# Splitting three of four block products of the second plain tile into float32r parts

## The chip, the cores and the metric

The kernel runs on 1 core of one Trainium2 chip. The metric is the device time of one execution in microseconds (us). Five engines work side by side, each through its own queue in order: TensorE (PE, with its weight loads PEld), VectorE (DVE), ScalarE (ACT), GpSimd (POOL) and SyncE (SP). SyncE issues plain DMAs, GpSimd the DMAs that add into their destination.

## The reference

One step of a decoder trunk in float32, over 512 new prompt rows and 8 sample rows (together NT = 520 columns here): a half-step SwiGLU FFN, a mixer of pooling heads and state-space heads, a second half-step FFN, a final norm. The change lies in the first FFN:

```python
def _rms_norm(x, g):
    xf = x.astype(jnp.float32)
    y = xf * lax.rsqrt(jnp.mean(xf * xf, axis=-1, keepdims=True) + EPS)
    return (y * g.astype(jnp.float32)).astype(x.dtype)

def _swiglu(x, wg, wu, wd):
    return (jax.nn.silu(x @ wg) * (x @ wu)) @ wd
...
    h = h + 0.5 * _swiglu(_rms_norm(h, ffn1_norm[l]), ffn1_w_gate[l], ffn1_w_up[l], ffn1_w_down[l])
```

x has 1024 features, the FFN 2816 hidden ones, which are 22 tiles of 128. The kernel keeps features on the 128 partitions: a matmul takes a 128x128 block of weights and 128 features of 260 columns (half of the 520).

## The kernel before

**Two forms of a product.** In float32 a product of a weight block and 260 columns is one matmul, which leaves two records in the profile. In split form (`mm3`, lines 121 to 126) weights and input are each held as a float32r number `hi` and a float32r remainder `lo`, and three float32r matmuls are added up: hi by hi (L122), hi by lo (L125), lo by hi (L126). The split needs work ahead: `hi` is a copy on ScalarE (L106), `lo` is either a subtraction on VectorE (L113) or a negated copy on ScalarE (L109) into which a DMA adds the weights from memory (L110, issued by GpSimd).

**Hidden tiles.** Most tiles of an FFN are done as units: a unit k (`load`, L329 to L353; `product`, L355 to L382) computes gate and up of a tile by seven block products instead of eight, which needs sums of weight blocks (L346 to L348) and of input blocks. `raw_k` is a unit's weights as loaded (L340), one of two buffers; `whi`, `wlo`, `shi`, `slo` are the split weights and sums, `A` and `BE` the PSUM banks, L380 the copies out of them. The names end in the tile's number and a letter for the part: `slo_1d` is the remainder of the second pair of sums of unit 1, and unit 4 comes after unit 1.

**Plain tiles.** The first two tiles of the first FFN (0 and 3; `second` is 3) are done in float32 without sums (`plain`, L299 to L312): for gate (u = 0) and up (u = 1), over eight feature blocks (j of 0 to 3, q of 0 and 1) and two column halves b, that is 32 float32 matmuls for a tile. Each half of the columns and of the features has a slot of `xg`: `xg[:, 0]` and `xg[:, 1]` are the columns of half 0 with the features of q = 0 and 1, `xg[:, 3]` and `xg[:, 2]` those of half 1. The tiles' weights are `raw_0` and `raw_3`; `raw_1` follows in the buffer of `raw_0`.

**The start of the program** (L544 to L565). In a loop over j, SyncE loads two feature blocks of x and a quarter of tile 0's weights; ScalarE scales them into `xg` (L188) and squares them (L162), VectorE adds the squares (L163); tile 0's matmuls follow; `prep_pair` makes the seven inputs of the units as `xth` (hi, L201) and `xtl` (lo, L202), slots 0 to 2 of which are `xg`'s slots 0 to 2. After the loop come the loads of tile 3's weights (L293), `scales` (the sum of squares over partitions by two float32 matmuls `psr`, L168, square root on ScalarE, L169, reciprocal on VectorE, L170, giving `r`), tile 3's matmuls, and `plain_out` for both tiles (L314 to L327): the gate's banks times `r` (L319), silu on ScalarE (L321), times `r` (L322), times the up banks (L324). `g_split` (L247 to L285) makes the hidden values' sums and parts for the down projection.

**What sets the order.** A list scheduler places the instructions of each engine by its own estimate of time; what stands under `high_priority` goes first when it can. An engine then works through its queue in that order, waiting by semaphores. PSUM tiles and SBUF buffers with the same tag rotate, so a new one waits for the readers of an old one. Before the change tile 3's gate has the tag "A" and its up the tag "BE", the tags of the units; `psr` has the tag "ps".

## Time and profile before

| | us |
|---|---|
| median of three runs | 984.8 (984.1 to 984.87) |
| the profiled execution | 984.47 |
| its span in the trace | 982.6 |
| granted TensorE clock, share of full | 0.997 |

In a page of the profile, busy time is listed by engine; a row of the timeline gives start, length, engine, line, operation, tile written and tiles read, shape and count, and in brackets idle time before it and what ended it. A row of the stretches gives start and end, length, then the busy time of PE, PEld, DVE, ACT and POOL with counts, the granted clock, the share of time that the 16 DMA engines were busy, and GB/s. A row of DMA issues gives the tile, the queue, the count, the size of each and the median time from issue to landing. The chain of work that ended last is followed back from the end of the program: at each step to what released it, or to the instruction before it on its engine.

### The profile page before, as it was taken

What the parts mean: (1) busy time and instruction counts of PE and PEld (TensorE: products, weight loads), DVE (VectorE), ACT (ScalarE), POOL (GpSimd) and SP (SyncE); (2) the same over time, 40 slices, a digit from 0 to 9 for tenths busy, and PEclk for the clock granted to TensorE, in tenths of its full rate; (3) what the DMA queues carried; (4) which work ended last, traced back from release to release, by engine and by line L of the source; (5) the groups of instructions that cost most, each with busy time, mean ns of one, the idle gap of its engine ahead of it and who ended that gap; (6) DMA issues with size and microseconds to landing.
All of it is one profiled execution on the core that took longest, in us unless ns stands there. A gap on an engine that the chain in (4) does not pass through costs nothing.

```text
span 982.6 us, 20242 instructions
## 1 busy us (share of the span) xinstructions
PE 951.5 (97%) x7636; PEld 927.4 (94%) x7636; DVE 877.8 (89%) x1624; ACT 678.2 (69%) x1263; POOL 217.9 (22%) x319
## 2 busy tenths in 40 slices
PE   7999999999999999999999999999999999999995
PEld 6899999999999999999899998989999999999995
DVE  7899899989989698788979987999999999999976
ACT  7677677677777475685754335678788888888864
POOL 0112211121121000157411000113333233233300
PEclk9999999999999999999999999999999999999998
DMA  5565766576566243262335232456687768767732
GB/s 182 161 172 114 191 161 143 133 186 175 124 149 165 65 148 119 87 210 86 115 120 165 96 115 90 106 152 164 164 213 185 183 156 223 190 155 189 190 91 88
DMA packets 63571, 145.46 MB, mean 148 GB/s; under 512 B 9257, under 2 KB 22505, under 8 KB 63473
## 3 DMA queue, kind: packets, MB, share of 16 engines
q1 hardware_dynamic: 41168, 103.78, 33.2%
q0 software_dynamic: 22304, 40.38, 22.5%
q8 instruction: 60, 0.98, 0.4%
q14 instruction: 39, 0.31, 0.1%
HBM read 136.80 MB, written 7.34 MB: 147 GB/s over the span
## 4 chain that ended last, share of the span: by engine, by line
PE 85%; DVE 8%; ACT 3%; issue 2%; DMA 1%; POOL 1%; SPq 0%; DVEq 0%; ACTq 0%
PE A L126 7%; PE A L122 7%; PE A L125 7%; PE BE L122 6%; PE BE L125 6%; PE BE L126 6%; PE P L311 3%; PE wo L122 2%; PE wo L125 2%; PE wo L126 2%; PE inz L122 2%; PE A2d L125 2%; PE A2d L126 2%; PE A1d L125 2%; PE A1d L126 2%
## 5 line engine op out<-in xcount | busy, mean ns | idle before, releaser
L380 ACT COPY ac<-A 128x260 f32<-128x260 f32 x123 | 45.1, 369 | 16.8 <-PE A L126 16.5
L311 PE MATMUL P<-xg_f,raw 128*128 128x260 f32 x192 | 45.9, 398 | 5.5 <-DMA raw<-in_w1gu 5.5
L346 DVE TENSOR_TENSOR s<-raw 128x1024 f32<-128x1024 f32 x41 | 49.8, 1216 | 1.4 <-DMA raw<-in_w2gu 1.4
L311 PEld LDWEIGHTS P<-xg_f,raw 128*128 128x128 f32 x192 | 37.5, 199 | 11.5 <-ACT xg_f L188 5.4
L943 POOL DMA_DIRECT2D out_nss<-hs x32 | 20.6, 643 | 79.2 <-DVE hs L961 74.0
L106 ACT CAST whi_wo<-raw_wo 128x1024 fp32r<-128x1024 f32 x12 | 12.5, 1046 | 36.5 <-issue 9.2
L125 PE MATMUL wo<-catg,whi_wo 128*128 128x260 f32 x128 | 36.4, 285 | 1.3 <-DVE catg L1092 1.3
L122 PE MATMUL wo<-catg,whi_wo 128*128 128x260 f32 x128 | 37.3, 292 | 0.3 <-DVE h L1061 0.3
L122 PE MATMUL inz<-xh_mx,whi_inz 128*128 128x260 f32 x128 | 36.8, 288 | 0.0
L122 PE MATMUL inx<-xh_mx,whi_inx 128*128 128x260 f32 x128 | 36.4, 285 | 0.0
L126 PE MATMUL wo<-catg,wlo_wo 128*128 128x260 f32 x128 | 36.3, 284 | 0.0
L126 PE MATMUL inz<-xh_mx,wlo_inz 128*128 128x260 f32 x128 | 36.2, 283 | 0.0
L126 PE MATMUL inx<-xh_mx,wlo_inx 128*128 128x260 f32 x128 | 36.2, 283 | 0.0
L125 PE MATMUL inz<-xl_mx,whi_inz 128*128 128x260 f32 x128 | 36.2, 283 | 0.0
L125 PE MATMUL inx<-xl_mx,whi_inx 128*128 128x260 f32 x128 | 36.1, 282 | 0.0
L392 DVE TENSOR_TENSOR tg<-BE,ac 128x520 f32<-128x520 f32 x41 | 28.3, 691 | 5.2 <-PE BE L126 5.2
L807 DVE SCALAR_TENSOR_TENSOR A<-U,h,A 128x544 f32<-128x544 f32 x36 | 28.0, 778 | 4.3 <-ACT A L805 3.3
L401 DVE TENSOR_TENSOR tg<-tg,r_f 128x520 f32<-128x520 f32 x41 | 28.4, 694 | 1.3 <-ACT tg L399 1.0
L398 DVE TENSOR_TENSOR tg<-tg,r_f 128x520 f32<-128x520 f32 x41 | 28.4, 692 | 0.1
L347 DVE TENSOR_TENSOR s<-s,raw 128x512 f32<-128x512 f32 x41 | 28.0, 682 | 0.0
L348 DVE TENSOR_TENSOR s<-s,raw 128x512 f32<-128x512 f32 x41 | 27.9, 681 | 0.0
L399 ACT ACTIVATE tg<-tg 128x520 f32<-128x520 f32 x41 | 26.1, 637 | 1.0 <-DVE tg L398 0.9
(1787 smaller groups left out, 4747.4 us busy)
## 6 DMA issues: line engine op xcount, KB each, us to landing
raw<-in_w2gu SPq DMA_DIRECT2D x44, 512.0 KB, 4.9
raw<-in_w1gu SPq DMA_DIRECT2D x42, 512.0 KB, 4.7
raw_1d<-in_w1d SPq DMA_DIRECT2D x24, 384.0 KB, 4.0
raw_2d<-in_w2d SPq DMA_DIRECT2D x24, 384.0 KB, 4.0
raw_wo<-in_w_out SPq DMA_DIRECT2D x12, 512.0 KB, 4.8
ab<-scr_acs SPq DMA_DIRECT2D x8, 512.0 KB, 4.4
h<-in_state_ssm SPq DMA_DIRECT2D x16, 256.0 KB, 3.8
raw_inz<-in_w_in SPq DMA_DIRECT2D x8, 512.0 KB, 4.1
```

What stands on the lines that cost most here:

```text
L122: first = nc.tensor.matmul(ps, whi, xhi, start=start, stop=False, **kw)
L125: nc.tensor.matmul(ps, whi, xlo, start=False, stop=False, **kw)
L126: nc.tensor.matmul(ps, wlo, xhi, start=False, stop=stop, **kw)
L311: nc.tensor.matmul(self.banks[f, u][b][:, :HB], ws(self.raw[f][:, u], j + 4 * q), xg[:, slot[q]], start=j == q == 0, stop=j == 3 and q == ...
L346: nc.vector.tensor_tensor(out=s1, in0=diag, in1=up0, op=ALU.add)
L347: nc.vector.tensor_tensor(out=s2[:, 0], in0=s1[:, 1], in1=raw[:, 0, :nb], op=ALU.add)
L348: nc.vector.tensor_tensor(out=s2[:, 1], in0=s2[:, 0], in1=raw[:, 0, nb : 2 * nb], op=ALU.add)
L380: nc.scalar.copy(keep, out[:, :HB])
L392: nc.vector.tensor_tensor(out=tg, in0=self.BE[k][:, :, :HB], in1=a, op=ALU.add)
L398: nc.vector.tensor_tensor(out=tg, in0=tg, in1=r, op=ALU.mult)
L401: nc.vector.tensor_tensor(out=tg, in0=tg, in1=r, op=ALU.mult)
L807: nc.vector.scalar_tensor_tensor(out=A[:, :n], in0=U[:, j : j + n], scalar=w(j), in1=A[:, :n], op0=ALU.mult, op1=ALU.add)
```

## The change

Tile 3 is computed by two new functions in place of `plain`. `plain_split` makes `phi` and `plo` of gate and up by two ScalarE instructions of 128x1024 each and one adding DMA of 512 KB each. `plain_mixed` leaves the combination of column half 1 with the features of q = 0 (slot 3 of `xg`) in float32, 8 matmuls, and does the other three in split form with `xth` and `xtl` slots 0 to 2, 72 matmuls: first hi with both inputs, then lo. The gate's banks stay "A", the up's become "ps". The new tiles live in the pool `xo`, which is released afterwards as before.

```diff
+        def plain_split(self, f, wpool):
+            src = ins[f"w{self.i}gu"]
+            for u in range(2):
+                hi, lo = (wpool.tile([P, 1024], F32R, tag=t, bufs=2, name=f"{t}{self.i}_{f}{u}") for t in ("phi", "plo"))
+                nc.scalar.copy(hi, self.raw[f][:, u])
+                nc.scalar.activation(out=lo, in_=self.raw[f][:, u], func=AF.Copy, scale=-1.0)
+                nc.gpsimd.dma_start(out=lo, in_=src[2 * f + u], accum_op=ALU.add)
+                self.w[f, u] = hi, lo
+
+        def plain_mixed(self, f, xgs):
+            for u, tag in enumerate(("A", "ps")):
+                self.banks[f, u] = [ps[0].tile([P, 512], F32, tag=tag, bufs=2, name=f"P{self.i}_{f}{u}{b}")
+                                    for b in range(2)]
+            n = KD // 2
+            for u in range(2):
+                for j in range(n):
+                    nc.tensor.matmul(self.banks[f, u][1][:, :HB], ws(self.raw[f][:, u], j), xgs[j][:, 3],
+                                     start=j == 0, stop=False, skip_group_check=True)
+            xth, xtl = self.nx[:2]
+            for low in (False, True):
+                for u in range(2):
+                    w = self.w[f, u][low]
+                    for j in range(n):
+                        for q, b in ((0, 0), (1, 0), (1, 1)):
+                            for x in (xth,) if low else (xth, xtl):
+                                nc.tensor.matmul(self.banks[f, u][b][:, :HB], ws(w, j + 4 * q), x[:, j, q + b],
+                                                 start=not low and x is xth and j == q == 0,
+                                                 stop=low and j == n - 1 and q == 1, skip_group_check=True)
...
     ffn1.plain_load(second)
     with tc.high_priority():
         ffn1.scales()
-    for u in range(2):
-        for j in range(KD // 2):
-            ffn1.plain(second, xg1[j], j, (u,))
+    ffn1.plain_split(second, xo)
+    ffn1.plain_mixed(second, xg1)
     xo.release()
```

## The prediction

> **What bounds the kernel now.** I read the page's totals, then the chain that ended last around the change, then each engine's timeline there.

> ```profile
> span 982.6 us, 20242 instructions
> PE 951.5 (97%) x7636; PEld 927.4 (94%) x7636; DVE 877.8 (89%) x1624; ACT 678.2 (69%) x1263; POOL 217.9 (22%) x319
> ```

> TensorE fills 97% of the span, so one expects every microsecond of matmul saved to be a microsecond of time. Around the second tile the chain says otherwise (start, length, what):

> ```profile
> 19.90 3.96 PE P L311 x18
> 23.88 4.54 DMA raw<-in_w1gu
> 28.44 1.05 ACT whi_1a L106
> ...
> 32.45 0.65 ACT tg L321
> 33.12 0.70 DVE tg L322
> ...
> 36.84 0.61 DVE s L348
> ...
> 37.51 3.52 DMA raw<-in_w1gu
> ...
> 42.94 0.39 PE BE L122
> ```

> The chain leaves TensorE when the first tile's last matmul frees `raw_0` (23.88), passes through the load of unit 1, ScalarE's splits and silu, VectorE's run from 33.12 to 37.45, the load of unit 4 (which waits for the buffer that L348 read last), ScalarE again, and comes back at 42.94. The second tile's matmuls are not on it; in TensorE's timeline they lie beside it:

> ```profile
> 24.56 1.04 PE L168 MATMUL psr_f<-acc_f,ones 128*128 128x260 f32 x4
> 25.44 11.64 PE L311 MATMUL P<-xg_f,raw 128*128 128x260 f32 x52
> 36.72 0.47 PE L122 MATMUL A<-xth_f,whi_1a 128*128 128x260 f32 x1
> ...
> 38.36 0.28 PE L122 MATMUL BE<-xth_f,shi_1c 128*128 128x260 f32 x1
> ...
> 40.99 0.28 PE L125 MATMUL A<-xtl_f,shi_1d 128*128 128x260 f32 x1
> ...
> 42.15 0.39 PE L122 MATMUL A<-xth_f,whi_4a 128*128 128x260 f32 x1 [0.76 <-ACT whi_4a L106]
> ```

> **What the change saves on TensorE.** A float32 matmul leaves two records: the two `psr` matmuls take 24.56 to 25.44, 0.44 us each. A split-form matmul takes 0.12 us (22 steps from 38.36 to 40.99). Of 32 float32 matmuls (14.1 us) 8 stay (3.5 us) and 24 become 72 (8.6 us): 1.9 us less, plus a wait of 0.2 us for a bank, which the "ps" banks avoid. (These are the `psr` banks: the second float32 group, 21 split matmuls behind `psr`'s end, needs them at 28.8, and the square roots have read them by 27.) The last record of the x52 row ends its slot at 36.9, so unit 1's first matmul can come at **34.8**. By the built order the first tile keeps its place: four float32 matmuls of the second lie inside it, as before, and it ends at 23.7, as the issue of the next load at 23.88 shows.

> **What the change adds on ScalarE.** Two copies and two scalings of 128x1024:

> ```profile
> 17.35 0.62 ACT L162 ACTIVATE sq_f<-h 128x520 f32<-128x520 f32 x1
> 17.88 0.83 ACT L201 CAST xth_f<-xg_f 128x780 fp32r<-128x780 f32 x1
> 18.61 1.05 ACT L201 CAST xth_f<-xd_f 128x1040 fp32r<-128x1040 f32 x1
> 22.81 1.06 ACT L201 CAST xth_f<-xd_f 128x1040 fp32r<-128x1040 f32 x1 [3.14 <-DVE xd_f L198]
> 23.89 1.28 ACT L169 ACT_TABLE_LOAD   x1
> 25.20 0.92 ACT L169 ACTIVATE r_f<-psr_f,eps 128x260 f32<-128x260 f32 x2
> ```

> A cast of this size costs 0.95 us from start to start (18.61 plus its 1.05, less the overlap of 0.1 seen between neighbours): 3.8 us. They stand in ScalarE's queue ahead of the square at 17.35, which with the three `xth` casts moves to 21.2 and after. The idle 3.14 us takes all but 0.6 of it; the table load then ends at 25.7. The sum of squares, a square of 0.62 us and an addition (0.70 us like L322 below, same size) after 21.2, is ready at 22.5, earlier than TensorE asks for it: both are hidden behind the first tile's matmuls, and would cost their overrun past 25.4 if ScalarE were later. `psr` itself, however, now stands behind 14 split matmuls: 23.69 + 14 x 0.12 = 25.4, **0.8 us later**, and so do the reciprocals.

> **What VectorE makes of it.** It gets no new instruction and loses none.

> ```profile
> 25.71 3.42 DVE L170 RECIPROCAL r_f<-r_f 128x260 f32<-128x260 f32 x2 [0.57 <-ACT r_f L169]
> ...
> 31.39 0.75 DVE L319 TENSOR_TENSOR tg<-P,r_f 128x260 f32<-128x260 f32 x2
> 33.12 0.70 DVE L322 TENSOR_TENSOR tg<-tg,r_f 128x520 f32<-128x520 f32 x1 [0.97 <-ACT tg L321]
> ...
> 42.12 0.69 DVE L113 TENSOR_TENSOR wlo_4a<-raw,whi_4a 128x512 fp32r<-128x512 f32 x1 [0.71 <-ACT whi_4a L106]
> ...
> 49.72 1.21 DVE L113 TENSOR_TENSOR slo_4d<-s,shi_4d 128x1024 fp32r<-128x1024 f32 x1
> 51.19 0.69 DVE L398 TENSOR_TENSOR tg<-tg,r_f 128x520 f32<-128x520 f32 x1
> 51.80 0.68 DVE L347 TENSOR_TENSOR s<-s,raw 128x512 f32<-128x512 f32 x1
> ```

> The 0.8 us and one L319 drawn forward (0.3) end the row at 31.39 at 32.5, still ahead of 33.12, when the silu arrives. That moment hangs on unit 1's load, not on the second tile: call its delay d. From there VectorE's order holds the same instructions up to `slo_4d`, plus one L319 (0.35) and one L398 (0.61, from 51.19 to 51.80), less the idle 0.71 at 42.12: unit 4's load now takes `raw_3`'s buffer, which TensorE reads last 37 split matmuls before 34.8, at 30.4, and not the one that L348 holds to 37.4. So `slo_4d` ends at 33.12 + 17.81 (33.12 to 50.93 before) - 0.71 + 0.96 = **51.2 + d**. TensorE wants it 112 matmuls after unit 1's first in both orders:

> ```profile
> 51.93 0.28 PE L126 MATMUL A<-xth_f,slo_4d 128*128 128x260 f32 x1
> ```

> Free of waits it would be there at 34.8 + 112 x 0.12 = 48.2; it has to wait until 51.2 + d. What was 2.1 us at 34.8 is 51.93 - 51.2 - d = **0.7 - d** here: most of the gain goes into waits for `slo_1d` and `slo_4d`. If VectorE's other gaps there close too (0.2: it is busy 16.89 of these 17.81 us, in the row below), it is 0.9 - d.

> **The new DMAs.** SyncE's order is unchanged. GpSimd issues the two adds ahead of `wlo_1a`'s, for which it sat idle until 30.33; issuing is hidden there. What they can cost is d.

> ```profile
> 23.75:29.50 5.75, 5.75 (x28) 4.99 (x27) 5.03 (x5) 3.38 (x6) 0.00 (x0) 1.00 0.61 185
> 31.50:35.50 4.00, 4.00 (x20) 3.48 (x19) 3.03 (x6) 3.05 (x4) 0.79 (x1) 1.00 0.84 128
> ...
> 33.12:50.93 17.81, 16.77 (x123) 15.83 (x122) 16.89 (x26) 10.75 (x18) 1.69 (x2) 1.00 0.56 156
> ...
> 30.33 0.99 POOL L110 DMA_DIRECT2D wlo_1a<-in_w1gu  x1 [29.88 <-ACT wlo_1a L109]
> ```

> The last but one column of the stretches is the DMA share (VectorE's busy time is the fourth figure): unit 1's load (1 MB) took 0.61 x 5.75 = 3.5 us of all 16 engines, two adds of 256 KB alone 0.84 x 4.00 = 3.4 us; one add of 512 KB is taken as much. The first, with its negated copy there at 19.4, is issued 0.3 us later and moves from about 21.2 on (the add issued at 30.33 moved in the stretch from 31.5) to 24.7; the second then has its 3.4 us at the very time of unit 1's load. How such neighbours share is seen where a pair of loads and a half-size add start together (the first answer is a pair alone at 37.5, the second one beside an add at 50; the last figure is us to landing):

> ```profile
> raw<-in_w1gu SPq DMA_DIRECT2D x2, 512.0 KB, 4.0
> ...
> raw<-in_w1gu SPq DMA_DIRECT2D x2, 512.0 KB, 4.4
> wlo_4b<-in_w1gu POOLq DMA_DIRECT2D x1, 256.0 KB, 6.3
> ```

> The loads land 0.4 us later; the add pays. I take **d = 0.4**, the nearest row; its ends are 0 and the whole 3.4 of the second add. For the second add itself: needed at 34.8 - 12 x 0.12 = 33.4, done at about 24.7 + 3.4 + 3.5 = 31.6 if all of the load goes first; were it late, TensorE has 3 us to lose ahead of `slo_4d`. The first is needed at 25.4 + 0.9 + 10 x 0.12 = 27.5 and alone on the engines until 24. [...]

> **After 51 us** TensorE is busy throughout again (15.00 of 15.00 us in the first row below), and the built order is that of before from some 100 us on, but for a few instructions late in the second FFN. The tightest hand-over left is `slo_5d`:

> ```profile
> 45.00:60.00 15.00, 15.00 (x126) 15.00 (x126) 14.54 (x21) 11.20 (x19) 2.54 (x3) 1.00 0.65 153
> ...
> 70.42 1.22 DVE L113 TENSOR_TENSOR slo_5d<-s,shi_5d 128x1024 fp32r<-128x1024 f32 x1
> ...
> 72.17 0.28 PE L126 MATMUL A<-xth_f,slo_5d 128*128 128x260 f32 x1
> ```

> It has 0.5 us to spare, more than the lead, and VectorE is 0.61 ahead by the L398. So the lead stays to the end. Sum: 0.7 - 0.4 = 0.3 us gained on the profiled execution's 984.47 us (span 982.6), giving 984.1; its median of three runs, 984.8, lies 0.3 higher, so **984.4**.

> **The rivals.** *The engines share evenly:* unit 1's first 512 KB are 1.75 us of work for all engines, 3.5 us for half of them. At the share of before (0.61) they took 2.9 us, at a full share they would take 1.75: the load loses 0.6 to 1.75 us, d = 1.2, the silu ends at 34.3, and the time is 984.8 + 1.2 - 0.7 = 985.3. For it: the add's rows are as long here as the load's, unlike those of the half-size adds. Against: 4.4 beside 4.0 above. *Slower, by one mechanism:* the second add, queued first, drains before the load gets the engines. Place: 24 to 28 us; price d - 0.7; it decides from d = 0.7 and can be measured from 2.7; at d = 3.4 the time is 987.5. For it: the add is issued 2 us ahead of the load. Against: in the rows above the add, issued first, landed last. *Faster, the matmul time counts in full:* if VectorE had 3 us to spare, TensorE would pass `slo_4d` at 48.2, 3.7 us early: 981.1. Against it: VectorE's only idle stretch of note there is the 0.71. That the change does not do what it says can be left out: the built order holds 8 float32 and 72 split matmuls.

> **How the numbers follow.** Forecast (d from 0 to 0.9): 0.60, own range 983.6 to 985.2. Even sharing: 0.17, 984.7 to 985.9. Add first: 0.14, 986 to 988. Full saving, or most of it: 0.09, 981.1 to 983. What a measurement of this kernel can tell from no change is about 0.2%, 2.0 us; the outer cases pass it nearly whole: faster 0.09, slower 0.13, within 0.78. The range leaves out most of the two outer cases: 983.0 to 986.6.

> **What would show it.** Right: unit 1's first matmul near 34.8; a wait of 1 to 2 us at `slo_1d` and a shorter one at `slo_4d`, both on VectorE; the silu between 33.1 and 34; `psr` near 25.4. Wrong: a wait for `plo` or `phi` in the second tile; unit 1's cast later than 29.5 (even sharing) or 31 (add first); no wait at `slo_4d`, with a lead over 2 us at 52 us.

## The result and the profile after

The changed kernel takes 987.58 us (median of 16 runs, 984.86 to 990.09) beside 984.88 us for the kernel before on the same chip (16 runs): a ratio of 1.0022, 95% interval 1.0012 to 1.0032. It is slower by about 2.7 us. The profiled execution of it took 988.75 us. The first lines of its page:

```profile
span 987.0 us, 20301 instructions
PE 952.3 (96%) x7660; PEld 928.5 (94%) x7660; DVE 878.3 (89%) x1624; ACT 682.7 (69%) x1267; POOL 219.8 (22%) x321
```

TensorE has 0.8 us more of busy time than before and 4.4 us more of span: it waits more. The chain of waits around the second tile of the changed kernel (start, length, what):

```profile
21.89 1.77 PE P L311 x8
23.67 7.28 DMA raw<-in_w1gu
30.98 1.05 ACT whi_1a L106
...
34.91 0.65 ACT tg L350
35.59 0.70 DVE tg L351
...
42.66 1.15 DVE slo_1d L113
43.85 0.39 PE A L126
...
52.30 1.15 DVE slo_4d L113
53.49 0.39 PE A L126
```

The chain runs as before, through unit 1's load, ScalarE's splits and silu and VectorE's run; but the load took 7.28 us where it took 4.54, and VectorE's run starts at 35.59 instead of 33.12. In TensorE's timeline the prediction's own marks are to be found:

```profile
25.16 1.04 PE L168 MATMUL psr_f<-acc_f,ones 128*128 128x260 f32 x4
...
34.71 0.28 PE L122 MATMUL A<-xth_f,whi_1a 128*128 128x260 f32 x1
...
43.85 0.39 PE L126 MATMUL A<-xth_f,slo_1d 128*128 128x260 f32 x1 [1.60 <-DVE slo_1d L113]
```

`psr` is at 25.16 (predicted 25.4), unit 1 begins at 34.71 (34.8), and the 2 us gained there are spent at `slo_1d` and its neighbours; TensorE comes to `slo_4d` at 53.49, 1.56 us later than before (51.93).

Where the rest went is seen when each matmul's start is set against the same matmul's start in the kernel before. The difference stays flat for long stretches and changes in a few places:

```
us in the program   after minus before   what changes there
 52                  +1.6                slo_4d, as above
359                  +0.1                before waits 1.35 us at its first dt matmul, after does not
432                  +1.5                after waits 0.9 us at pm, before does not
475 to 481           +3.1                after's TensorE clock is halved for 3.41 us
911                  +4.3                after waits 1.0 us for slo_2d_2d, behind a load that landed 9.2 us after its issue
```

The waits of TensorE between 355 and 482 us, first of the changed kernel, then of the kernel before:

```profile
PE pb L1004 <- DVE U L749: 1.0, 1, 1.0
PE pm L125 <- DVE catp L882: 0.9, 1, 0.9
PE px L1012 <- DVE xdt L1036: 0.7, 1, 0.7
```

```profile
PE dt L737 <- DVE dt_v L757: 1.4, 1, 1.4
PE px L984 <- DVE xdt L1008: 0.7, 1, 0.7
PE pb L976 <- DVE U L721: 0.6, 1, 0.6
PE yd L1027 <- DVE U L719: 0.4, 1, 0.4
```

All of these lie 300 us and more behind the edited lines, in a stage (the mixer) whose instructions the change does not touch. So the loss of this execution has three parts: 1.6 us at the place of the change, 1.5 us in the mixer, and 1.2 us near 911 us. The last did not come again below.

### The profile page after: what moved, and what is told of

It is laid out like the page before. It is cut to its first block, busy times and chain, and to the rows that moved or that the text cites. A ratio compares the mean times of both kernels' runs of the same rounds, so it can differ in the third digit from the quotient of the medians.

```text
span 987.0 us, 20301 instructions
## 1 busy us (share of the span) xinstructions
PE 952.3 (96%) x7660; PEld 928.5 (94%) x7660; DVE 878.3 (89%) x1624; ACT 682.7 (69%) x1267; POOL 219.8 (22%) x321
## 3 DMA queue, kind: packets, MB, share of 16 engines
q1 hardware_dynamic: 41168, 103.78, 33.4%
## 4 chain that ended last, share of the span: by engine, by line
PE 77%; DVE 11%; ACT 4%; DMA 4%; issue 3%; POOL 1%; SPq 0%; DVEq 0%; ACTq 0%
PE A L126 7%; PE A L122 7%; PE A L125 7%; PE BE L122 6%; PE BE L125 6%; PE BE L126 5%; PE P L311 3%; PE wo L122 2%; PE wo L125 2%; PE wo L126 2%; PE inz L122 2%; PE inz L125 2%; PE inz L126 2%; PE A1d L125 2%; PE A1d L126 2%
## 5 line engine op out<-in xcount | busy, mean ns | idle before, releaser
L106 ACT CAST whi_wo<-raw_wo 128x1024 fp32r<-128x1024 f32 x12 | 12.5, 1045 | 36.7 <-issue 10.3
L125 PE MATMUL wo<-catg,whi_wo 128*128 128x260 f32 x128 | 36.4, 285 | 1.3 <-DVE catg L1120 1.2
L122 PE MATMUL inz<-xh_mx,whi_inz 128*128 128x260 f32 x128 | 37.5, 293 | 0.1
L122 PE MATMUL wo<-catg,whi_wo 128*128 128x260 f32 x128 | 37.3, 292 | 0.3 <-DVE h L1089 0.3
L311 PE MATMUL P<-xg_f,raw 128*128 128x260 f32 x128 | 31.8, 404 | 5.4 <-DMA raw<-in_w1gu 5.4
L125 PE MATMUL inz<-xl_mx,whi_inz 128*128 128x260 f32 x128 | 36.8, 288 | 0.0
L126 PE MATMUL inz<-xh_mx,wlo_inz 128*128 128x260 f32 x128 | 36.8, 287 | 0.0
L122 PE MATMUL inx<-xh_mx,whi_inx 128*128 128x260 f32 x128 | 36.4, 285 | 0.0
L126 PE MATMUL wo<-catg,wlo_wo 128*128 128x260 f32 x128 | 36.3, 284 | 0.0
L126 PE MATMUL inx<-xh_mx,wlo_inx 128*128 128x260 f32 x128 | 36.2, 283 | 0.0
L125 PE MATMUL inx<-xl_mx,whi_inx 128*128 128x260 f32 x128 | 36.1, 282 | 0.0
L311 PEld LDWEIGHTS P<-xg_f,raw 128*128 128x128 f32 x128 | 25.4, 202 | 9.4 <-ACT xg_f L188 5.4
## 6 DMA issues: line engine op xcount, KB each, us to landing
raw<-in_w2gu SPq DMA_DIRECT2D x44, 512.0 KB, 5.1
raw<-in_w1gu SPq DMA_DIRECT2D x42, 512.0 KB, 4.7
raw_wo<-in_w_out SPq DMA_DIRECT2D x12, 512.0 KB, 4.4
ab<-scr_acs SPq DMA_DIRECT2D x8, 512.0 KB, 4.1
h<-in_state_ssm SPq DMA_DIRECT2D x16, 256.0 KB, 3.9
raw_inz<-in_w_in SPq DMA_DIRECT2D x8, 512.0 KB, 4.1
```

The lines of the kernel that those rows point to most:

```text
L122: first = nc.tensor.matmul(ps, whi, xhi, start=start, stop=False, **kw)
L125: nc.tensor.matmul(ps, whi, xlo, start=False, stop=False, **kw)
L126: nc.tensor.matmul(ps, wlo, xhi, start=False, stop=stop, **kw)
L311: nc.tensor.matmul(self.banks[f, u][b][:, :HB], ws(self.raw[f][:, u], j + 4 * q), xg[:, slot[q]], start=j == q == 0, stop=j == 3 and q == ...
```

## The experiments

Theory 1: the second add sits in the DMA engines when unit 1's load starts, delays it, and VectorE's run hands the delay to `slo_4d`. Its rivals: the engines share evenly whatever the order (theory 2); the loss is made late, by another order (theory 3). Theories 4 and 5, on the mixer, were formed from the first runs. All results in one table, so that the readings below can be short: the median, the ratio to the kernel before with its 95% interval, runs in which the mean granted clock was 0.995 or lower (the others have 0.996 or 0.997), and from the profile the time from issue to landing of `raw_1`'s first half, TensorE's start at `slo_4d`, its wait at `dt`, the landing time of the store `scr_dt`, and TensorE's wait at `pm`.

```
                   us   ratio               low clock  raw_1  slo_4d  dt   scr_dt  pm
before          984.8                        1 of 98   4.54   51.93   1.4  1.30    -
before_again    984.05 (one run)                       4.60   52.04   1.4  1.31    -
after           987.58  1.0022 [12, 32]     10 of 16   7.28   53.49   -    2.13    0.9
after_again     986.07  1.0014 [05, 23]      6 of 12   6.02   52.71   -    1.95    0.6
no_add_1        985.14  1.0007 [-06, 20]     7 of 12   5.28   50.62   -    2.21    1.5
late_add        986.15  1.0014 [05, 23]      3 of 12   5.77   52.76   -    2.27    0.7
later_add       986.96  1.0019 [05, 32]      5 of 10   3.80   54.28   -    2.19    0.8
vec_lo          987.19  1.0024 [10, 38]      8 of 10   4.26   52.39   -    2.44    2.0
be_banks        990.31  1.0062 [49, 74]      3 of 6    7.14   55.40   1.4  2.59    1.1
before_adds     988.75  1.0045 [33, 57]      4 of 5    5.88   55.30   1.4  1.30    -
before_ps       982.87  0.9984 [-24, -07]    2 of 10   4.41   51.20   -    1.30    -
before_pad      983.59  0.9990 [-18, -01]    2 of 12   3.59   51.02   -    1.76    0.8
after_pad       984.49  0.9995 [-13, 04]     1 of 11   5.38   51.67   -    1.44    -
after_pad40     985.15  1.0011 [01, 20]      2 of 10   6.33   52.89   -    1.51    0.5
after_pad256    991.11  1.0070 [55, 85]      4 of 4    8.43   55.95   -    2.23    1.1
best            984.93  1.0000 [-10, 09]     1 of 11   3.58   52.53   -    1.33    -
```

(Intervals in steps of 0.0001 from 1. The runs come from several chips, so rows are compared by their ratios, each of which is to the kernel before on the same chip. The low clock is a mean over a run and does not tell where the clock fell. One of the eleven runs of before_ps took 2,843 us and tells nothing of the kernel; its clock is left out of the count.)

### The changed kernel and the kernel before, once more

> The changed kernel once more, unedited. Theory 1 (the adds hold back unit 1's load, everything else of the loss comes and goes from run to run): raw_1's first half again lands about 7.3 us after its issue, TensorE is again at slo_4d at 53.5 us (1.56 later than before), but the steps of the pair of profiles at 432, 477 and 911 us (1.5 us, 1.5 us and 1.2 us) do not all come again. Theory 3 (the loss is made late, by the other order in the second FFN and by the mixer's phase): the steps at 477 and 911 us come again, each by over 1 us. Time by both: 1.5 to 3 us above the kernel before.

> The kernel before once more, for a second profile of it: all theories expect TensorE at slo_4d within 0.5 us of 51.93, the wait of 1.35 us at dt near 359 us, none at pm near 432 us, and a clock that stays at 1.00 from its rise near 10 us to the last 10 us.

The wait for `slo_4d` came again, at 52.71 with a load of 6.02 us: 0.8 us lost instead of 1.56. The add and the load do not meet alike in every run: here the add was issued at 21.34 and the load at 24.16, in the first profile at 21.98 and 23.67, so less of the add was left. The halved clock and the late load at 911 us did not come again in this profile, but the low clock did in 6 of the 12 runs; over both sets it is 16 of 28, with a median of 987.6 us in those 16 and 985.2 us in the other 12. The kernel before has a low clock in 1 run of 98. So theory 3 in its plain form (an order that costs the same in each run) falls, and something in the changed kernel makes a halved clock likely.

With the clock whole, the mixer costs almost nothing. Set against the kernel before, matmul by matmul, this second profile is 0.8 us late at `slo_4d`, 0.7 early behind `dt`, 0.3 late behind `pm` and 0.6 late at the end: the wait that went and the wait that came nearly cancel. The 12 runs without a low clock, at 985.2 us, lie 0.3 to 0.4 us above the medians of the kernel before on the same chips (984.88 and 984.81). So beyond `slo_4d` it is mainly the low clock that makes the loss.

### Without the second add

```diff
-                nc.gpsimd.dma_start(out=lo, in_=src[2 * f + u], accum_op=ALU.add)
+                if u == 0:
+                    nc.gpsimd.dma_start(out=lo, in_=src[2 * f + u], accum_op=ALU.add)
```

> Leaves out the second adding DMA (the low half of the second tile's second weight half then holds only the negated copy, so this part of the computation is wrong); all other instructions stay. Theory 1: the first add (3.4 us of the engines from 21.2) is out by 24.7 to 25.6, the load lands 4.5 to 5.3 us after its issue (after: 7.3), slo_4d ends at 51.2 to 51.7, TensorE is 0.2 to 0.7 us ahead of the kernel before there, and the time is 0 to 1 us below it. Theory 3: the load lands as early, but the time stays over 1 us above the kernel before. Rival (the delay is not the adds' doing but that of ScalarE's splits or psr): slo_4d stays near 53.4.

TensorE's row at `slo_4d` in this kernel:

```profile
50.62 0.39 PE L126 MATMUL A<-xth_f,slo_4d 128*128 128x260 f32 x1 [0.71 <-DVE slo_4d L113]
```

With one add gone, TensorE is 1.3 us ahead of the kernel before instead of 1.6 behind. Part of this is the start: the first rise of the clock comes between 8.2 and 11.2 us from run to run (at 9.91 in the first profile of the changed kernel and at 10.25 in that of the kernel before), and here unit 1's load is issued 1.1 us earlier. So the profiles are better compared from that issue on. d is then the silu product's start behind it, against 9.24 us in the kernel before; the lead is TensorE's at `slo_4d`, against 28.05 us:

```
              load issued   silu product   slo_4d     d     lead    0.9 - d
before          23.88          33.12       51.93
after           23.67          35.59       53.49     2.68   -1.77    -1.78
after_again     24.16          34.81       52.71     1.41   -0.50    -0.51
no_add_1        22.81          32.72       50.62     0.67   +0.24    +0.23
after_pad       23.74          33.76       51.67     0.78   +0.12    +0.12
after_pad40     24.02          34.98       52.89     1.72   -0.82    -0.82
```

The prediction's second formula, 0.9 - d, holds to 0.01 us in these five profiles, the ones in which VectorE's order up to `slo_4d` is that of the changed kernel (the last two come below). So in them d is all that the place of the change decides. Without the second add it falls to 0.67 and the lead is positive: that the loss comes from ScalarE's copies or from `psr` is out, for both are still there. And yet the time is not below that of the kernel before: 7 of 12 runs have the low clock, and TensorE waits 1.5 us at `pm`. The first part of the loss is the second add's; the second part does not need it.

### The second add issued later

```diff
+                with tc.issue_after(casts[6]) if u else nullcontext():   # later_add: casts[7]
                     nc.scalar.activation(out=lo, in_=self.raw[f][:, u], func=AF.Copy, scale=-1.0)
```

(`casts` holds ScalarE's `xth` casts of L201 in order; 6 and 7 are the last pair's two.)

> The second add is kept, but its negated copy is put behind the first of the last three xth casts on ScalarE, so that the add is issued at about 24.3 instead of 21.98, 0.6 us after unit 1's load. Same work on every engine. Theory 1 (what is queued first drains first): the load lands 4.5 to 5.3 us after its issue, plo_31 lands near 32, slo_4d ends at 51.2 to 51.7, the time is 0 to 1 us below the kernel before. Theory 2 (engines share evenly whatever the order): the load shares with the add and lands 6 to 7 us after its issue, slo_4d ends at 52.4 to 53, the time is 0.5 to 1 us above the kernel before. Theory 3: over 1 us above whatever the load does.

> The second add's negated copy is put behind all three last xth casts on ScalarE, so that the add is issued at about 25.5 us, 1.5 us after unit 1's load (in late_add it still came 1.2 us ahead of it). Theory 1 (what is queued first drains first): the load's first half lands 4.3 to 4.8 us after its issue, the silu ends by 33.5, slo_4d ends at 51.3 to 52.2; plo_31 lands at 32 to 34 and TensorE may wait for it by up to 1 us ahead of unit 1, which it can afford. Theory 2 (even sharing): the load lands 5.4 us or more after its issue and slo_4d ends at 52.3 or later, as in late_add.

late_add missed its aim: the add was issued at 22.95, still 1.2 us ahead of the load, and all came out about as in after_again; its times tell nothing between theories 1 and 2. later_add does. Its DMA issues, from three windows of the DMA view that hold one issue each, in the order of their issue at 24.51, 24.77 and 24.88 us (the last figure is us to landing):

```profile
raw<-in_w1gu SPq DMA_DIRECT2D x1, 512.0 KB, 3.8
...
plo<-in_w1gu POOLq DMA_DIRECT2D x1, 512.0 KB, 7.0
...
raw<-in_w1gu SPq DMA_DIRECT2D x1, 512.0 KB, 7.4
```

The half of the load that was issued 0.26 us before the add lands in 3.8 us, the half that was issued 0.11 us after it in 7.4. They do not share: from 25.5 to 27 us the load has 87.8% of the engines and the adds nothing, from 28 to 29.5 the add has 102.2% and the load 1.4% (a packet counts whole where it starts, so a share can pass 100%). So theory 2 falls. A lead of a tenth of a microsecond does not always decide: in the row at 50 us that the prediction used, the add was issued at 49.87, between the halves of the load (49.60 and 49.97), and both halves landed ahead of it. For the time the later add was no help, because the silu stands on ScalarE behind the splits of both halves, and the clock was halved at 38.50, behind a step of 3.41 us in which TensorE was idle for 2.25. How the changed kernel's engines were divided is seen in its DMA view from 24 to 26, 26 to 26.5, 27.5 to 28 and 28 to 30 us (packets, MB, share of 16 engines; q0 carries the adds, q1 the load, issued at 23.67):

```profile
q0 software_dynamic: 116, 0.41, 106.0%
...
q0 software_dynamic: 22, 0.09, 90.2%
q1 hardware_dynamic: 4, 0.02, 8.7%
...
q0 software_dynamic: 16, 0.05, 55.1%
q1 hardware_dynamic: 19, 0.08, 40.4%
...
q1 hardware_dynamic: 209, 0.79, 97.3%
q0 software_dynamic: 17, 0.02, 5.5%
```

Up to 26 us the load moves nothing; then its share climbs from 9% to 40% in 2 us and to 97% after 28, as the adds run out. In late_add the step is shorter: up to 26.5 us the load moves nothing, and from 27 to 27.5 it has 72.2%. The two do not advance together: these rows show the load waiting for adds that were issued 1.2 us or more ahead of it.

### The adds alone, in the kernel before

```diff
+    ffn1.extra_adds(second, xo)     # two negated copies and two adding DMAs into tiles that nobody reads
     for u in range(2):
         for j in range(KD // 2):
             ffn1.plain(second, xg1[j], j, (u,))
```

> The kernel before, with the two negated copies on ScalarE and the two adding DMAs into tiles that nobody reads; the second tile stays in float32. This is the transfers' cost alone, without the saving on TensorE. Theory 1: unit 1's load lands 6 to 7.3 us after its issue, the silu and all behind it come 1.3 to 2.5 us later, TensorE is at slo_4d at 53.2 to 54.4 us (before: 51.93), the time is 1.3 to 2.5 us above the kernel before. Theory 2 (even sharing): d = 1.2, at slo_4d at 53.1, 1.2 us above. Rival (the loss comes from the split form, not from the adds): at slo_4d at 52 us, time as before.

VectorE's silu product comes at 34.31 (33.12 without the adds), and TensorE to `slo_4d` at 55.30: 3.4 us lost where 1.3 to 2.5 were expected. TensorE waits 0.9 us for `whi_1a` and 1.8 us for `whi_4a`, and a second loss comes behind the wait, a halved clock:

```profile
43.56:46.98 3.42, 3.40 (x15) 3.40 (x16) 3.42 (x6) 1.15 (x3) 0.85 (x1) 0.50 0.84 231
```

(The granted clock is 0.50 over 3.42 us.) That the adds alone cost time is shown, and the rival that blames the split form is out. How they cost it is not told here: d is 1.27 us, near the 1.2 of theory 2 as well. The loss was set too low because no theory reckoned with the clock.

### VectorE instead of the adds

```diff
-                nc.scalar.activation(out=lo, in_=self.raw[f][:, u], func=AF.Copy, scale=-1.0)
-                nc.gpsimd.dma_start(out=lo, in_=src[2 * f + u], accum_op=ALU.add)
+                nc.vector.tensor_tensor(out=lo, in0=self.raw[f][:, u], in1=hi.bitcast(F32), op=ALU.subtract)
```

> Both low halves of the second tile by one VectorE subtraction each (1.2 us by the 128x1024 rows) in place of ScalarE's negated copies and the adding DMAs. VectorE gets 2.4 us more before the reciprocals, of which 1.4 us fall into its idle stretch at 20.8; ScalarE gets 1.9 us less. Theory 1: no add, so the load lands 4.5 us after its issue; the reciprocals end by about 31, the silu still ends at 33.1, slo_4d ends at 51.2 and the time is 0.7 us below the kernel before. Rival: VectorE's subtractions come late for the reciprocals and move the row of L351 past 33.1 by up to 1 us, and the lead is gone. Theory 3: over 1 us above the kernel before in any case.

The load lands in 4.26 us, as theory 1 says, but the rival holds for the rest. VectorE's timeline in this kernel:

```profile
19.42 2.35 DVE L319 TENSOR_TENSOR plo<-raw,phi 128x1024 fp32r<-128x1024 f32 x2
...
28.01 3.41 DVE L170 RECIPROCAL r_f<-r_f 128x260 f32<-128x260 f32 x2 [0.55 <-ACT r_f L169]
...
34.36 1.30 DVE L350 TENSOR_TENSOR tg<-tg,r_f 128x520 f32<-128x520 f32 x2
```

The reciprocals begin 1.3 us later than in the changed kernel, and the silu product follows at 34.36. The transfer's cost has become VectorE's. At `slo_4d` this kernel comes 0.5 us later than the kernel before, but its time is 2.4 us above that of the kernel before: it has the longest wait at `pm` (2.0 us) and the low clock in 8 of 10 runs. The mixer's part is by far the larger here.

### The banks of the second tile

Theory 4 came from the wait at `dt`, which the kernel before has and the first four kernels with the split form do not: all of these take two `ps` banks for the second tile where the kernel before takes a BE pair.

```diff
 be_banks (in the changed kernel):
-            for u, tag in enumerate(("A", "ps")):
+            # u = 0 from two A banks, u = 1 from one BE pair, as before
 before_ps (in the kernel before):
-                    if f and u == 0:
-                        bs = [ps[0].tile([P, 512], F32, tag="A", bufs=2, name=f"{n}{b}") for b in range(2)]
+                    if f:
+                        bs = [ps[0].tile([P, 512], F32, tag=("A", "ps")[u], bufs=2, name=f"{n}{b}") for b in range(2)]
```

> The changed kernel, with the second tile's up half in one BE pair of banks, as in the kernel before, instead of two ps banks; nothing else is edited. The BE pairs are taken in turn, so the changed kernel's later tiles stand in the other pair of the two. Theory 4 (the turn of the pairs decides the rest of the loss): TensorE again waits 1.3 to 1.4 us at its first dt matmul near 359 us, as in the kernel before, and no longer at pm near 432 us (0.6 to 0.9 us in the two profiles of the changed kernel); the granted clock no longer halves for 3.4 us near 477 us in about half of the runs (16 of 28), but in 1 of 33 as before; the loss at slo_4d stays, 0.9 to 1.6 us, or a few tenths more for the wait for a bank; time 0.5 to 1.2 us above the kernel before. Rival (the halved clock comes from TensorE's delay at slo_4d, or by chance): no wait near 359 us or the clock halves in half of the runs all the same; time 1.3 to 2.7 us above.

> The kernel before, with the second tile's up half in two ps banks instead of a BE pair; no split form, no adds. Theory 4: the wait of 1.35 us at dt near 359 us goes, a wait of 1 to 2 us at pm near 432 us comes, the clock halves near 477 us in a third or more of the runs, and the time rises by 0.3 to 1 us though the stage of the change does the same work. Rival: nothing moves, time within 0.3 us of the kernel before and the clock halves in 1 run of 33.

Half of theory 4 holds. be_banks waits 1.4 us at `dt` again, before_ps does not, and over all sixteen profiles the wait is there in the four whose kernel takes no extra `ps` tile and in none of the other twelve (in the pad kernels below, the extra tiles are those of the pads). The other half falls: be_banks waits at `pm` as well, before_ps does not. be_banks also pays 3.1 us of wait for `whi_1a` early on, so its time says little. before_ps keeps what it gained: 982.87 us, ratio 0.9984 (0.9976 to 0.9993), faster than both kernels, with two words of code changed and none of the split form. (It is the lowest ratio here, but before_pad's 0.9990 below is not clear of it.) Its waits of TensorE from 355 to 482 us:

```profile
PE px L984 <- DVE xdt L1008: 0.7, 1, 0.7
PE pb L976 <- DVE U L721: 0.6, 1, 0.6
```

### The instruction fetch

What lies behind the wait at `pm`? The chain from 398 to 436 us in the changed kernel is a row of small transfers through DRAM:

```profile
403.57 2.13 DMA scr_dt<-dts
...
406.40 5.90 DMA sdt<-scr_dt
...
417.64 2.02 DMA scr_acs<-ach
...
421.51 7.24 DMA ab<-scr_acs
...
430.89 0.62 ACT catp L881
```

Its first link, a store of 0.5 KB, lands in 1.30 to 1.31 us in the four profiles without the split form taken until then, and in 1.95 to 2.59 in the six with it. The DMA view of the changed kernel from 403.5 to 405 us, and that of the kernel before from 403 to 404.9, say why:

```profile
q8 instruction: 1, 0.02, 4.0%
...
scr_dt<-dts SPq DMA_DIRECT2D x1, 0.5 KB, 2.1
```

```profile
scr_dt<-dts SPq DMA_DIRECT2D x1, 0.5 KB, 1.3
```

One packet of 16,384 bytes on the instruction queue, 0.96 us long, starts at 403.72 and meets the store. In the kernel before, the fetch of this place comes at 408.5, behind it. Such a packet comes every 16 us or so (by the medians 15.7 us in the changed kernel and 16.0 in the kernel before). The trace of the kernel before has 60 packets on this queue and 15,272 matmuls and weight loads, on average 255 for each packet. The changed kernel has 48 more of these instructions, and its 25th packet, the one at 403.72, starts 4.8 us earlier than the 25th of the kernel before; its others start between 6.6 us earlier and 4.3 us later than theirs. Theory 5 is that this shift is the second part of the loss. Its test adds instructions that do nothing, at the start, where TensorE waits for the first data:

```diff
     ffn_psum("ppf1")
+    z = cst.tile([P, 16], mybir.dt.bfloat16, tag="z", name="z")
+    nc.vector.memset(z, 0.0)
+    for n in range(2):
+        zb = bank(f"pad{n}")
+        for _ in range(20):          # after_pad40: 10, after_pad256: 64
+            nc.tensor.matmul(zb[:16, :16], z, z, start=True, stop=True)
```

> The kernel before with 40 matmuls of 16x16 zeros (80 instructions for TensorE, results unread) at the very start, where TensorE waits for the first loads; nothing else. They move TensorE's later 16 KB instruction fetches about 5 us earlier: in the kernel before one is recorded at 408.5 us, in the changed kernel at 403.7 us, where it meets the 0.5 KB store scr_dt (1.30 us to land in four profiles without the split form, 1.95 to 2.59 us in five with it). Theory 5 (the changed number of TensorE instructions moves the fetch onto this store, and the late store delays VectorE's catp, on which TensorE waits at pm): the fetch comes at 403 to 404.5 us, scr_dt takes about 2.1 us, TensorE waits 0.3 us or more at pm near 432 us, and the time rises by 0.3 to 1.5 us although no work of the program is changed. Rival (the wait at pm belongs to the split form itself): scr_dt 1.3 us, no wait at pm, time within 0.3 us of the kernel before.

> The changed kernel with the same 40 tiny matmuls at the start: the fetch recorded at 403.7 us should come near 398.7 us, ahead of the store. Theory 5: scr_dt 1.3 us, the wait at pm gone or under 0.3 us, the clock halves near 477 us in fewer runs than 16 of 28, and the time falls by 0.5 to 1.5 us against the changed kernel, to 984.8 to 986 us (0 to 1.2 us above the kernel before: the loss at slo_4d stays, the wait at dt near 359 us stays away). Rival: scr_dt near 2.1 us and the wait at pm as in the changed kernel; time 1.3 to 2.7 us above the kernel before.

In after_pad the store does as theory 5 says: fetch at 397.0, store 1.44 us, no wait at `pm`, low clock in 1 run of 11. The ratio is 0.9995, where the unpadded rerun has 1.0014: the 40 tiny matmuls take 1.16 us of TensorE's time and make the program faster.

Not all of this gain is the store's. Counted from the issue of unit 1's load, TensorE is also 0.6 us earlier at `slo_4d` (a lead of +0.12 against -0.50), and the pad moved an earlier fetch as well. That one starts at 26.04 and 26.89 us in the two profiles of the changed kernel, while unit 1's load is under way, and at 18.3 in after_pad, ahead of the load. What such a fetch costs the load is seen where no adds are: `raw_1`'s first half lands in 4.26 to 4.60 us in the four profiles with the fetch beside it (before, before_again, before_ps, vec_lo), and in 3.59 in before_pad, which has the fetch at 15.6. How much of after_pad's 0.6 us is this fetch's is open, for after_pad40 has it at 19.7 and still a load of 6.33 us.

before_pad is a mixed case: the later fetch came at 400.8, 0.4 us ahead of the store instead of on it; the store took 1.76 us, TensorE waits 0.8 us at `pm`. But TensorE is 0.9 us earlier at `slo_4d`, and the wait at `dt` (1.4 us) is gone with the pad's two `ps` banks. Neither was foreseen, and the sum is a gain of 1.3 us.

As the pads changed more things (TensorE busy earlier, two banks, the early fetch), the fetch at the store had to be moved by itself:

> The changed kernel with 128 tiny matmuls (256 instructions for TensorE, one 16 KB fetch) at the start instead of 40 (80 instructions). If it is the place of the fetch in the program that matters, one whole fetch more brings it back to where it was: Theory 5: a fetch at 403 to 404.5 us, scr_dt 1.9 to 2.6 us, a wait at pm of 0.5 us or more, the clock halved in a quarter or more of the runs, time 985.5 to 987.5, as the changed kernel and 1 to 2.5 us above the version with 40. Rival (after_pad gained because TensorE works earlier at the start, by the two ps banks that the tiny matmuls take, or by chance): as after_pad, scr_dt under 1.5 us, no wait at pm, 984 to 985.

> The changed kernel with 20 tiny matmuls (40 instructions): the fetch should come about 2.5 us earlier than in the changed kernel, near 400.5 to 401.2 us, and be done by 402.5, 1 us ahead of the store. Theory 5: scr_dt 1.3 to 1.5 us, no wait at pm over 0.3 us, time within 0.7 us of the kernel before, as after_pad. Rival (any collision with the loads before the store is as bad): the wait at pm stays and the time is 985.5 to 987.5.

256 instructions more, about one packet's worth by the 255 above, bring a fetch back to the store: it starts at 406.3, 0.2 us after the store's issue. The DMA view of after_pad256 from 405.9 to 408 us, and then TensorE's waits from 425 to 482 us:

```profile
q8 instruction: 1, 0.02, 2.6%
...
scr_dt<-dts SPq DMA_DIRECT2D x1, 0.5 KB, 2.2
```

```profile
PE pb L1010 <- DVE U L755: 1.1, 1, 1.1
PE pm L125 <- DVE catp L888: 1.1, 1, 1.1
```

The slow store and the wait are back, with the pads and their banks in place: for these it is the fetch's place that counts. The time, 991.11 us, and the low clock in 4 of 4 runs cannot be read in the same way, for this kernel also loses early. The second add is issued only 0.67 us ahead of unit 1's load, which lands in 8.43 us; ScalarE's second square root stands behind the splits of this load, and TensorE waits 2.4 us for it; the clock is halved at 33.90 and once more at 481.04, behind `pm`. after_pad40 stands between: the fetch starts at 402.5, 0.6 us ahead of the store, which takes 1.51 us, but the next one, at 417.0, meets the chain's second store, `scr_acs`, which takes 2.54 us (1.81 in the kernel before). The wait is 0.5, the time 985.15.

### All pieces together

```diff
 after_pad, and in plain_split, for u == 1:
-                nc.scalar.activation(...); nc.gpsimd.dma_start(..., accum_op=ALU.add)
+                nc.vector.tensor_tensor(out=lo, in0=self.raw[f][:, u], in1=hi.bitcast(F32), op=ALU.subtract)
```

> The changed kernel with three edits: the low part of the second weight half by one VectorE subtraction in VectorE's idle 1.41 us at 20.8 (no second add, one negated copy less on ScalarE), and the 40 tiny matmuls at the start. Theories 1 and 5 together: the load lands 4.5 to 5.3 us after its issue, TensorE is at slo_4d 0.7 to 1.2 us ahead of the kernel before, the wait of 1.35 us at dt stays away, scr_dt takes 1.3 us and TensorE does not wait at pm: 2 to 2.7 us below the kernel before, 982 to 983. Rival: the subtraction delays the reciprocals as in vec_lo, and the time is at best that of the kernel before.

The load lands in 3.58 us, the silu product comes at 32.03, and TensorE does not wait at `dt` or `pm`; but 984.93 is not 982 to 983. VectorE stands idle for 2.09 us ahead of `wlo_4a`: unit 4's load is now issued at 30.49, right behind the add of `wlo_1b` (30.33), and lands in 6.9 us. The same collision as at first, one unit later: TensorE is at `slo_4d` 0.6 us behind the kernel before and not 0.7 to 1.2 ahead. A second loss stands behind the mixer's known waits, near 488 us:

```profile
PE px L1021 <- ACT X L846: 1.0, 1, 1.0
```

after_pad has this wait too; the kernel before, the changed kernel and after_pad40 do not have it. What brings it about stays open.

## Why the prediction was wrong

Most steps at the place of the change held: unit 1's first matmul (34.71), `psr` (25.16), ScalarE's copies in the idle time, raw_4's load drawn forward to 30.53, the waits on VectorE at `slo_1d` and `slo_4d`, and the formula for the lead at `slo_4d`, in its form with VectorE's gaps closed, 0.9 - d.

**The step that failed first** is "I take d = 0.4, the nearest row". Measured from the load's issue, d was 2.68 us, and 1.41 in the second profile. In the row chosen the load's first half was issued 0.27 us ahead of the add, and not behind it as the argument against the slower rival says ("the add, issued first, landed last"); the case at hand was an add issued 1.7 us ahead of the load. The DMA views of the changed kernel and of late_add show what a load behind such an add gets: nothing up to 26 and 26.5 us, which is 2.3 us behind its issue in both, and in the changed kernel 97.3% of the engines only after 28 us, when the adds have all but run out. The prediction had this mechanism as its slower rival ("the second add, queued first, drains before the load gets the engines") and gave it 0.14. Also, the first add was put on the engines until 24.7; it landed at 25.61, so that both adds stood in the way. The sign named for this rival, a cast of unit 1 later than 31, was just missed at 30.98; the second profile's d of 1.41 is near the 1.2 of even sharing, so the rows of shares decide between the two and not d.

**The step that failed second** is "So the lead stays to the end", with the built order as its reason. An equal order is not an equal time: with the extra `ps` banks the wait at `dt` went (a gain of 1.4 us that no step foresaw), by the moved instruction fetch a wait at `pm` came, and 16 of 28 runs had a low clock (2.4 us by the medians); the one halving that a profile of this kernel shows ahead of its last 10 us stands behind `pm`, at 477.54. The prediction counted what the new DMAs cost as d alone, and what 48 more TensorE matmuls cost as their time alone; that the instruction fetches move with them (the one at 408.54 us to 403.72) stood in no rival. At 987.58 the result lies in the add-first rival's range of 986 to 988, but that is in part luck: that mechanism by itself is worth 1.8 us at `slo_4d` in the first profile and 0.5 in the second (the leads above), and after_pad, which has both adds too, ends at the time of the kernel before. (The forecast's own sum is off by a rounding, 984.47 - 0.3 being 984.2; that plays no part.)

What is not settled: why the first dt matmul's wait depends on the `ps` tiles taken 300 us earlier was only read from the pattern over sixteen profiles (which bank it inherits was not traced); where the clock fell in the runs without a profile is not on record; and the late load at 911 us in the first profile of the changed kernel (9.2 us, 8.1 in the second) is left as it is.

## What to carry to other kernels

A transfer that is "hidden" has to be checked against the next critical load that is issued behind it: here two adds of 512 KB, the second issued 1.7 us ahead of a load, had the engines first (from 24 to 26 us the load moved nothing), which cost that load up to 2.7 us, and a saving of 2 us was gone. Where a change adds or removes instructions on TensorE, see where the instruction queue's packets lie in the DMA view around the small transfers of a serial chain; if one has come to lie on such a transfer, a few idle instructions at the start can move it off: here 40 tiny matmuls took the fetch at 403.7 us to 397.0, and an earlier one from 26.0 to 18.3. Before a difference of 0.2% is put down to the edited lines, set the start of each matmul against the kernel before: the steps show where the time really changes.

## What the runs showed of the hardware

```profile
474.13:477.54 3.41, 1.70 (x18) 1.05 (x14) 3.41 (x12) 3.41 (x9) 2.51 (x8) 1.00 0.03 5
477.54:480.95 3.41, 3.39 (x15) 3.39 (x16) 3.41 (x7) 2.98 (x8) 2.06 (x2) 0.50 0.52 197
```

TensorE is busy for 1.70 of 3.41 us in the first and runs at 0.50 in the next. In be_banks the emptiest step kept its clock:

```profile
476.93:480.34 3.41, 1.91 (x20) 1.22 (x19) 3.41 (x14) 3.41 (x11) 1.77 (x8) 1.00 0.00 0
480.34:483.75 3.41, 3.26 (x25) 3.02 (x26) 3.41 (x7) 3.41 (x9) 2.72 (x2) 1.00 0.66 193
```

Between 465 and 485 us, all five profiles that have a step with 1.66 us or more of idle time (1.66 to 1.78) show the halved clock in the step behind it, and all others (at most 1.50) do not. Ahead of 45 us, later_add, before_adds and after_pad256 have a fall behind steps with 2.25, 2.09 and 2.39 us. It is no sharp rule: in be_banks the step at 29.78 us has 1.76 us of idle time, and in vec_lo that at 36.59 has 1.64, and the clock stays at 1.00 behind both. The wait at `pm` by itself costs 0.5 to 2 us; in the changed kernel it also comes with other waits behind it: 1.0 us at `pb` and 0.7 at `px`, close together, where the kernel before has 0.7, 0.6 and 0.4 us at `px`, `pb` and `yd`. That the closer waits more often fall into one step, and so make a low clock likelier, fits the profiles, but was not tested by itself.

**A small store beside an instruction fetch landed later.** In the changed kernel a packet of 16 KB, 0.96 us long, started 0.15 us behind the issue of a 0.5 KB store, which landed in 2.13 us instead of 1.30 (1.95 to 2.59 over the kernels with the split form and no pad). Where the fetch lay went with the number of instructions ahead of it: with 40 tiny matmuls more it started at 397.0 and the store landed in 1.44 us, with 128 it started 0.2 us behind the store's issue and the store took 2.23. The load beside a fetch took longer too: the 512 KB of `raw_1`'s first half, without adds beside it, landed in 4.26 to 4.60 us with a fetch (before, before_again, before_ps, vec_lo) and in 3.59 without (before_pad).
